# Attention probabilities made once in float32 and multiplied with float32 values, in a hybrid attention, long-convolution and expert layer

## The chip, the cores and the metric

The kernel runs on one core of a Trainium2 chip. The metric is the device time of one execution in microseconds (us), taken as the median of several runs of the same program. Each core has a matrix engine (TensorE, PE in the profile, with its weight loads shown apart as PEld), a vector engine (VectorE, DVE), an activation engine (ScalarE, ACT), a general engine (GpSimd, POOL) and a queue that issues transfers (SyncE, SP). Each engine takes its instructions in the order in which the program has them.

## The reference: what is computed

One layer over 1024 latent tokens of width 1024 with 256 context tokens. Tokens are normalised and modulated, projected to queries (8 heads of 64), keys and values (2 shared heads), three streams of a long convolution and two gates. Windowed attention and a two-step long convolution run side by side, their outputs are merged by the gates and projected, and a 32-expert layer (4 experts for each token) follows. The part that the change touches is the windowed attention of one block of 128 queries:

```python
s_loc = jnp.einsum('bqhgd,bshd->bhgqs', q_blk, k_blk).astype(jnp.float32) * scale
s_loc = jnp.where(valid, s_loc, -jnp.inf)
s_c = jnp.einsum('bqhgd,bchd->bhgqc', q_blk, k_ctx).astype(jnp.float32) * scale
p = jax.nn.softmax(jnp.concatenate([s_loc, s_c, s_sink], axis=-1), axis=-1).astype(v.dtype)
o = (jnp.einsum('bhgqs,bshd->bqhgd', p[..., :span], v_blk)
     + jnp.einsum('bhgqc,bchd->bqhgd', p[..., span:span + n_ctx], v_ctx))
```

Everything is float32. A query block looks at three key blocks of 128 around it (two at the ends) and at two blocks of context, and each head has a sink, a logit without a value.

## The kernel before

The program is written as generators that are advanced in turn, and a scheduler with its own model of durations then sets the order of each engine's instructions. Most products are float32 in effect: each operand is split into a float16 part and a float16 remainder, and three float16 matmuls (high by high, high by low, low by high) are summed in PSUM.

**Where the time goes, in order.** Up to about 300 us filters, layer norms and the convolution's input projections; from 300 to 664 us the long convolution (`hyena`, mostly on DVE) mixed with the value projection (`vproj`), the query and key projections (`qk`) and the gates (`gate`, line 821 by way of `proj`); from 664 to 884 us the attention, 4 query blocks alone and 4 mixed with the first half of the merge (`merge`, line 1102); from 884 to 928 us the second half of the merge; then the output projection (line 1143), the routing, and from about 1050 us the experts to the end.

**`vproj`** projects 10 tiles of 128 tokens (8 latent, 2 context). Line 890 (ACT) writes the high part of the values to `V`, line 891 (DVE) the remainder, both out of the same PSUM tile, of which there are three (`mm`). For each tile and shared head `V` holds 64 remainders, 64 high parts and a column of ones (129 float16 columns).

**`attn(g, i)`** treats the four heads of one shared head `g` for query block `i`; there are 16 such units, two for each block. Lines 997 and 998 make the scores with queries as rows, for the maximum alone (lines 999 to 1003, DVE); line 1007 (DVE) spreads the maxima to `Dm`. Then for each key block (4 or 5 of them, 76 in all units) lines 1013 to 1016 make the scores again, keys as rows and the four heads side by side (512 columns), less the maximum, in a PSUM tile `st` (`ff`, three of them). Line 1018 (ACT) takes the exponential to float16 (`ph`), line 1019 (ACT) the same exponential to float32 (`pe`), line 1020 (DVE) the difference to float16 (`pl`). Lines 1026 to 1028 multiply with the values, with the probabilities as weights (128 keys by 128 queries, loaded anew for each matmul) and the values as the moving operand (65 or 64 columns), into `O` (`tp`): three matmuls for each head and key block. The column of ones gives the denominators, which lines 1030 to 1032 (DVE) apply. After both units of a block four transposes (line 1041) bring the result to `aT`.

Two other float32 products on TensorE are of use below. Line 573 has a weight of 2 columns and 128 moving columns, and line 1061 has a weight of 128 columns and 1 moving column. Line 902 and line 1041 are float32 transposes.

Of the kernel before, what the change touches and what calls it, by code (L numbers as in the profile page):

```python
# [13 lines left out]
F32 = mybir.dt.float32  # L14
F16 = mybir.dt.float16
# [3 lines left out]
AF = mybir.ActivationFunctionType  # L19
ALU = mybir.AluOpType  # L20
# [494 lines left out]
class PhaseA:  # L515
# [364 lines left out]
    def vproj(s):  # L880
        nc=s.nc
        w=s.wsplit(640)
        nc.gpsimd.memset(s.V[:,:,:,128:129],1.0)
        for t in range(10):
            p=s.pmm()[:,:128]; i=0
            for k in range(8):
                for a,b in ((0,0),(0,1),(1,0)):
                    nc.tensor.matmul(p,s.hx[a][:,k,t*128:(t+1)*128],w[b][:,k,:],start=i==0,stop=i==23); i+=1
            pv=p.rearrange("p (g d) -> p g d",g=2)
            nc.scalar.activation(s.V[:,t,:,64:128],pv,AF.Copy,scale=2.**-6)  # L890
            nc.vector.scalar_tensor_tensor(s.V[:,t,:,0:64],pv,2.**-6,s.V[:,t,:,64:128],op0=ALU.mult,op1=ALU.subtract)
            if t%2==1: yield

    def hyena(s,hf,o,z):
# [65 lines left out]
class PhaseA2(PhaseA):  # L960
# [21 lines left out]
    def attn(s,wk,g,i,att):  # L982

        nc=s.nc
        qs=slice(i%2*128,i%2*128+128); hs=slice(4*g,4*g+4)
        loc=[j for j in (i-1,i,i+1) if 0<=j<8]
        keys=[(j*128,j) for j in loc]+[(1024,8),(1152,9)]
        mx=wk.tile([128,2,4],F32,name="mx",bufs=2)
        p2=s.pmm().rearrange("p (h k) -> p h k",h=4)
        nl=len(loc)+1  # L990
        for h in range(4):
            p=s.pmm()
            qh=s.Q2[i//2][0][0:64,4*g+h,qs]
            for n,(o,j) in enumerate(keys):
                dst=p[:,n*128:(n+1)*128] if n<nl else p2[:,h,:]
                msk=s.mlt if j==i-1 else s.mgt if (j==i+1 and j<8) else None
                nc.tensor.matmul(dst,qh,s.K2[0:64,g,o:o+128],start=True,stop=msk is None)  # L997
                if msk is not None: nc.tensor.matmul(dst,s.idb,msk,start=False,stop=True)
            nc.vector.tensor_reduce(out=mx[:,0,h:h+1],in_=p[:,:nl*128],axis=AX.X,op=ALU.max)
        nc.vector.tensor_reduce(out=mx[:,1,:],in_=p2,axis=AX.X,op=ALU.max)  # L1000
        m=wk.tile([128,4],F32,name="m4",bufs=2); mb=wk.tile([128,4],BF,name="mb",bufs=2)
        nc.vector.tensor_tensor(m,mx[:,0],mx[:,1],op=ALU.max)
        nc.vector.tensor_tensor(mb,m,s.sink[:,hs],op=ALU.max)
        nc.vector.tensor_tensor(m,s.sink[:,hs],mb,op=ALU.subtract)
        es=wk.tile([128,4],F32,name="es",bufs=2); nc.scalar.activation(es,m,AF.Exp)
        Dm=wk.tile([128,4,128],BF,name="Dm",bufs=2)
        nc.vector.tensor_tensor(Dm,s.nidb[:,None,:].to_broadcast([128,4,128]),mb[:,:,None].to_broadcast([128,4,128]),op=ALU.mult)
        O=s.ptp()[:,:4*65].rearrange("p (h c) -> p h c",h=4)
        P=[]
        for n,(o,j) in enumerate(keys):  # L1010
            st=s.pff().rearrange("p a b -> p (a b)").rearrange("p (h q) -> p h q",h=4)
            msk=s.mgt if j==i-1 else s.mlt if (j==i+1 and j<8) else None
            nc.tensor.matmul(st,s.K2[:,g,o:o+128],s.Q2[i//2][0][:,hs,qs],start=True,stop=False)
            nc.tensor.matmul(st,s.K2[:,g,o:o+128],s.Q2[i//2][1][:,hs,qs],start=False,stop=False)
            if msk is not None: nc.tensor.matmul(st,s.idb,msk[:,None,:].to_broadcast([128,4,128]),start=False,stop=False)
            nc.tensor.matmul(st,s.onb,Dm,start=False,stop=True)
            pe=wk.tile([128,4,128],F32,name="pe",bufs=2); ph=wk.tile([128,4,128],F16,name="ph",bufs=6); pl=wk.tile([128,4,128],F16,name="pl",bufs=6)
            nc.scalar.activation(ph,st,AF.Exp)
            nc.scalar.activation(pe,st,AF.Exp)
            (nc.gpsimd if n in s.plp else nc.vector).tensor_tensor(pl,pe,ph,op=ALU.subtract)  # L1020
            P.append((j,ph,pl))
        L=len(P)-1
        for h in range(4):
            d=O[:,h]
            for n,(j,ph,pl) in enumerate(P):
                nc.tensor.matmul(d,ph[:,h,:],s.V[:,j,g,64:129],start=n==0,stop=False)
                nc.tensor.matmul(d[:,0:64],ph[:,h,:],s.V[:,j,g,0:64],start=False,stop=False)
                nc.tensor.matmul(d,pl[:,h,:],s.V[:,j,g,64:129],start=False,stop=n==L)
        den=wk.tile([128,4],F32,name="den",bufs=2)
        nc.vector.tensor_tensor(den,O[:,:,64],es,op=ALU.add)  # L1030
        nc.vector.reciprocal(den,den)
        nc.vector.tensor_tensor(att[:,4*g:4*g+4,:],O[:,:,0:64],den[:,:,None].to_broadcast([128,4,64]),op=ALU.mult)
# [208 lines left out]
def build(nc,tc,A,out,dbg=None,nexp=32):  # L1241
    with ExitStack() as es:
# [3 lines left out]
        with ExitStack() as ea:  # L1246
            ec=ExitStack(); a=PhaseA2(nc,tc,A,ea,ec,dp); a.accD=accD; a.out=out; a.idb_,a.mcp=m.idf,m.cp
            a.HTd=dp.tile([2,128,4,1024],F16,name="HTd"); a.rowD=dp.tile([3,1024],F32,name="rowD")
            a.usepool,a.poolw=False,False
            a.V=a.cp.tile([128,10,2,129],F16,name="V")  # L1250
            E=lambda name,side="left": tc.tile_pool(name=name,bufs=1,side=side)
            eF,eK,eL,eP,eZ,eS,eQ,eA,eT=[ExitStack() for _ in range(9)]
            dq=lambda n:A[n].rearrange("h b a c k -> b h (a c k)").rearrange("b h (a c k) -> b h a c k",a=8,c=2)
# [139 lines left out]
```

## Time and profile before

| | us |
|---|---|
| three runs | 2492.09, 2493.93, 2496.49 (median 2493.93) |
| profiled execution | 2488.39, span 2486.6 |
| PE busy | 2196.3 (88%) |
| DVE busy | 2139.5 (86%) |
| ACT busy | 1466.0 (59%) |
| the three value matmuls, 304 each, lines 1026 to 1028, in 664 to 884 us | 36.3, 36.2 and 35.2 busy |
| the two exponentials, 76 each, in 664 to 884 us | 45.4 and 45.2 busy |
| the difference `pl`, 76, in 664 to 884 us | 51.3 busy |

Busy time of an engine is the union of its instructions' records. A matmul's record runs from its start to its result, so matmuls that follow each other closely overlap: what one of them occupies is read from the distance of the starts, not from its duration.

### The profile page before, as it was taken

The page shows a single profiled execution, that of the slowest core. Times are in us where ns is not written, and L with a number is a line of the kernel's source. Part 1 is how long each engine was busy: PE and PEld are TensorE (multiplying, and loading weights), DVE is VectorE, ACT ScalarE, POOL GpSimd, SP SyncE. Part 2 cuts the span into 40 slices and gives each one's busy share as a digit, 9 for nine tenths or more (in the row PEclk, how much of TensorE's full clock was granted, in tenths as well). Part 3 has the DMA queues.
Part 4 walks back from the last instruction along what each step waited for, and adds up shares of the span by engine and source line. Part 5 has one row for each costly group of instructions (what it writes and reads, how often), then busy time and mean ns, then how long its engine had stood idle before and what let it go on. Part 6 is the DMA issues. An engine that isn't in the chain of part 4 may idle for free.

```text
span 2486.6 us, 60718 instructions
## 1 busy us (share of the span) xinstructions
PE 2196.3 (88%) x25072; PEld 1650.7 (66%) x25073; DVE 2139.5 (86%) x4004; ACT 1466.0 (59%) x2185; POOL 347.6 (14%) x224
## 2 busy tenths in 40 slices
PE   7888999997498999569899989998989999999991
PEld 4555465444254544345666768898989999999991
DVE  6878897987978846869889988999999999999984
ACT  3543344223246413356867758697877878788882
POOL 0000001000000005201021021322041111221114
PEclk9899999999599999779898989998999999999995
DMA  8425546543314233288999989999999999999984
GB/s 288 136 85 171 194 139 180 168 163 114 87 18 136 81 119 129 90 280 280 306 293 310 313 286 332 330 331 329 340 327 349 337 343 336 353 349 358 349 273 154
DMA packets 520402, 594.25 MB, mean 239 GB/s; under 512 B 16708, under 2 KB 472332, under 8 KB 520118
## 3 DMA queue, kind: packets, MB, share of 16 engines
q1 hardware_dynamic: 493432, 508.27, 61.0%
q0 software_dynamic: 13152, 43.69, 6.9%
q10 hardware_dynamic: 13534, 38.35, 4.5%
q8 instruction: 198, 3.24, 0.5%
q14 instruction: 86, 0.70, 0.1%
HBM read 532.95 MB, written 57.29 MB: 237 GB/s over the span
## 4 chain that ended last, share of the span: by engine, by line
PE 45%; DVE 25%; DMA 8%; issue 7%; ACT 4%; POOL 3%; SPq 0%; DVEq 0%; POOLq 0%; ACTq 0%
PE acc L347 26%; DVE wl L317 8%; PE mm L1102 4%; PE mm L821 3%; DVE bf L731 3%; DMA g<-rows,gi 2%; PE acc L344 2%; DMA raw<-in_exp_w 2%; ACT wh L315 2%; DMA bf<-Hd 1%; DMA accD<-yr,si 1%; PE mm L997 1%; DVE sl L394 1%; PE yt L434 1%; DVE sg L393 1%
## 5 line engine op out<-in xcount | busy, mean ns | idle before, releaser
L317 DVE SCALAR_TENSOR_TENSOR wl<-raw,wh 128x1024 f16<-128x1024 f32 x768 | 910.0, 1216 | 56.4 <-ACT wh L315 53.5
L315 ACT ACTIVATE wh<-raw 128x1024 f16<-128x1024 f32 x768 | 768.2, 1049 | 183.1 <-PE acc L347 73.4
L347 PEld LDWEIGHTS <-wh 128*128 128x128 f16 x9984 | 785.6, 99 | 93.2 <-issue 17.4
L347 PE MATMUL acc<-xT,wh 128*128 128x80 f16 (+18 forms) x6656 | 718.7, 236 | 4.1 <-DVE yT L421 2.2
L347 PE MATMUL acc<-xT,wl 128*128 128x112 f16 (+19 forms) x3328 | 638.7, 235 | 0.4 <-issue 0.4
L347 PEld LDWEIGHTS <-wl 128*128 128x128 f16 x4992 | 493.0, 99 | 46.8 <-issue 10.7
L347 PE MATMUL acc<-ah,wh 128*128 128x112 f16 (+19 forms) x1664 | 329.8, 239 | 12.4 <-ACT ah L403 5.6
L347 PE MATMUL acc<-al,wh 128*128 128x112 f16 (+19 forms) x1664 | 330.6, 239 | 6.6 <-DVE al L404 6.5
L347 PE MATMUL acc<-ah,wl 128*128 128x112 f16 (+19 forms) x1664 | 330.4, 240 | 0.0
L821 PE MATMUL mm<-hx,wh 128*128 128x512 f16 (+1 forms) x1072 | 325.6, 382 | 4.6 <-DVE hx L636 4.0
L437 POOL DMA_INDIRECT accD<-yr,si x49 | 127.5, 2602 | 667.6 <-ACT yr L436 416.7
L821 PE MATMUL mm<-hx,wl 128*128 128x512 f16 x536 | 205.2, 383 | 2.7 <-DVE wl L808 2.7
L821 PEld LDWEIGHTS <-wh 128*128 128x128 f16 x1072 | 105.9, 99 | 118.6 <-issue 7.5
L277 POOL DMA_INDIRECT g<-rows,gi x44 | 119.4, 2714 | 462.2 <-DVE tf L266 418.5
L731 DVE TENSOR_TENSOR bf<-bf 128x256 f32<-128x256 f32 (+1 forms) x272 | 131.5, 541 | 0.3
L422 ACT ACTIVATE yT<-acc,bc,g2s 128x112 f32<-128x112 f32 (+19 forms) x208 | 97.7, 482 | 27.3 <-PE acc L347 27.2
L821 PEld LDWEIGHTS <-wl 128*128 128x128 f16 x536 | 53.0, 99 | 70.3 <-issue 10.2
L403 ACT ACTIVATE ah<-sl 128x64 f16<-128x64 f32 (+18 forms) x140 | 56.7, 409 | 52.8 <-DVE sl L399 52.5
L344 PEld LDWEIGHTS <-wl 128*128 128x128 f16 x1152 | 79.6, 99 | 12.0 <-issue 10.5
L344 PEld LDWEIGHTS <-wh 128*128 128x128 f16 x1152 | 81.4, 104 | 6.8 <-DVE yT L421 4.7
L393 DVE TENSOR_SCALAR sg<-acc,bc 128x112 f32<-128x112 f32 (+19 forms) x208 | 75.4, 378 | 11.4 <-PE acc L347 11.4
L394 DVE TENSOR_SCALAR sl<-acc,bc 128x112 f32<-128x112 f32 (+19 forms) x208 | 75.3, 377 | 10.9 <-PE acc L347 10.5
(399 smaller groups left out, 3574.6 us busy)
## 6 DMA issues: line engine op xcount, KB each, us to landing
raw<-in_exp_w SPq DMA_DIRECT2D x384, 1024.0 KB
wr<-in_w_in SPq DMA_DIRECT2D x34, 512.0 KB
t<-in_w_mod ACTq DMA_DIRECT2D x32, 512.0 KB
bf<-in_dec SPq DMA_DIRECT2D x32, 256.0 KB
Hd<-bf ACTq DMA_DIRECT2D x32, 256.0 KB
bf<-Hd SPq DMA_DIRECT2D x32, 256.0 KB
Gd<-t ACTq DMA_DIRECT2D x16, 512.0 KB
gt<-Gd SPq DMA_DIRECT2D x32, 256.0 KB
```

Source lines behind the costliest of these rows:

```text
L277: nc.gpsimd.indirect_dma_start(out=g[:cs].rearrange("p a d -> p (a d)"),out_offset=None,in_=s.rows,in_offset=bass.IndirectOffsetOnAxis(ap= ...
L315: else: nc.scalar.activation(wh[:,o],raw[:,o],AF.Copy,scale=sc)
L317: else: nc.vector.scalar_tensor_tensor(wl[:,o],raw[:,o],64.0,wh[:,o],op0=ALU.mult,op1=ALU.subtract)
L344: nc.tensor.matmul(ps_,wh,x[k],start=k==0,stop=False); nc.tensor.matmul(ps_[:,0],wl,x[k][:,0],start=False,stop=k==7)
L347: nc.tensor.matmul(ps_,a,b,start=n==0,stop=n==23); n+=1
L393: nc.vector.tensor_scalar(g[:,j],pg[:,j],bc[:,f:f+1],448.0,op0=ALU.add,op1=ALU.min)
L394: nc.vector.tensor_scalar(l[:,j],pl[:,j],bc[:,8+f:9+f],512.0,op0=ALU.add,op1=ALU.min)
L422: nc.scalar.activation(y,py,AF.Identity,bias=bc[:,16+m:17+m],scale=s.g2s[:,m:m+1])
L437: st=nc.gpsimd.indirect_dma_start(out=s.accD,out_offset=bass.IndirectOffsetOnAxis(ap=si[:cs,:1],axis=0),in_=yr[:cs],in_offset=None,compute ...
L731: (nc.gpsimd if pool and s.usepool else nc.vector).tensor_tensor(o,a,b,op=op)
L821: nc.tensor.matmul(p,w[a][:,k,:],s.hx[b][:,k,o],start=i==0,stop=i==23); i+=1
L1102: nc.tensor.matmul(p,w[a_][:,k,m*128:(m+1)*128],X[x][:,k,o] if b==0 else X[x][:,k,:],start=n==0,stop=n==11); n+=1
```

## The change

`V` becomes float32 with 65 columns (64 values and the ones): line 890 writes the float32 values and line 891 is gone. In `attn` lines 1018 and 1020 are gone: the exponential is taken once, to float32, in six buffers in place of two. The three float16 matmuls of a head and a key block become one matmul with a float32 weight (128 by 128) and 65 float32 moving columns.

```diff
--- before.py
+++ after.py
@@ -880,15 +880,14 @@
     def vproj(s):
         nc=s.nc
         w=s.wsplit(640)
-        nc.gpsimd.memset(s.V[:,:,:,128:129],1.0)
+        nc.gpsimd.memset(s.V[:,:,:,64:65],1.0)
         for t in range(10):
             p=s.pmm()[:,:128]; i=0
             for k in range(8):
                 for a,b in ((0,0),(0,1),(1,0)):
                     nc.tensor.matmul(p,s.hx[a][:,k,t*128:(t+1)*128],w[b][:,k,:],start=i==0,stop=i==23); i+=1
             pv=p.rearrange("p (g d) -> p g d",g=2)
-            nc.scalar.activation(s.V[:,t,:,64:128],pv,AF.Copy,scale=2.**-6)
-            nc.vector.scalar_tensor_tensor(s.V[:,t,:,0:64],pv,2.**-6,s.V[:,t,:,64:128],op0=ALU.mult,op1=ALU.subtract)
+            nc.scalar.activation(s.V[:,t,:,0:64],pv,AF.Copy,scale=2.**-6)
             if t%2==1: yield
 
     def hyena(s,hf,o,z):
@@ -1014,18 +1013,12 @@
             nc.tensor.matmul(st,s.K2[:,g,o:o+128],s.Q2[i//2][1][:,hs,qs],start=False,stop=False)
             if msk is not None: nc.tensor.matmul(st,s.idb,msk[:,None,:].to_broadcast([128,4,128]),start=False,stop=False)
             nc.tensor.matmul(st,s.onb,Dm,start=False,stop=True)
-            pe=wk.tile([128,4,128],F32,name="pe",bufs=2); ph=wk.tile([128,4,128],F16,name="ph",bufs=6); pl=wk.tile([128,4,128],F16,name="pl",bufs=6)
-            nc.scalar.activation(ph,st,AF.Exp)
+            pe=wk.tile([128,4,128],F32,name="pe",bufs=6)
             nc.scalar.activation(pe,st,AF.Exp)
-            (nc.gpsimd if n in s.plp else nc.vector).tensor_tensor(pl,pe,ph,op=ALU.subtract)
-            P.append((j,ph,pl))
+            P.append((j,pe))
         L=len(P)-1
         for h in range(4):
-            d=O[:,h]
-            for n,(j,ph,pl) in enumerate(P):
-                nc.tensor.matmul(d,ph[:,h,:],s.V[:,j,g,64:129],start=n==0,stop=False)
-                nc.tensor.matmul(d[:,0:64],ph[:,h,:],s.V[:,j,g,0:64],start=False,stop=False)
-                nc.tensor.matmul(d,pl[:,h,:],s.V[:,j,g,64:129],start=False,stop=n==L)
+            for n,(j,pe) in enumerate(P): nc.tensor.matmul(O[:,h],pe[:,h,:],s.V[:,j,g,:],start=n==0,stop=n==L)
         den=wk.tile([128,4],F32,name="den",bufs=2)
         nc.vector.tensor_tensor(den,O[:,:,64],es,op=ALU.add)
         nc.vector.reciprocal(den,den)
@@ -1247,7 +1240,7 @@
             ec=ExitStack(); a=PhaseA2(nc,tc,A,ea,ec,dp); a.accD=accD; a.out=out; a.idb_,a.mcp=m.idf,m.cp
             a.HTd=dp.tile([2,128,4,1024],F16,name="HTd"); a.rowD=dp.tile([3,1024],F32,name="rowD")
             a.usepool,a.poolw=False,False
-            a.V=a.cp.tile([128,10,2,129],F16,name="V")
+            a.V=a.cp.tile([128,10,2,65],F32,name="V")
             E=lambda name,side="left": tc.tile_pool(name=name,bufs=1,side=side)
             eF,eK,eL,eP,eZ,eS,eQ,eA,eT=[ExitStack() for _ in range(9)]
             dq=lambda n:A[n].rearrange("h b a c k -> b h (a c k)").rearrange("b h (a c k) -> b h a c k",a=8,c=2)
```

Lines behind 890 move up by one, and behind the exponential by seven, so that line 1026 of before is line 1021 of after. The scheduler also moves other instructions between 300 and 930 us; on PE the last 32,625 instructions, with the whole expert part among them, stand in the same order in both.

On PE, at the end of a unit's value product, before: `ph` and `pl` are the probabilities, `att` the finished block, `K` and `Q` the next scores.

```order
L1026 LDWEIGHTS ph
L1026 MATMUL tp<-V,ph 128x65
L1027 LDWEIGHTS ph
L1027 MATMUL tp<-V,ph 128x64
L1028 LDWEIGHTS pl
L1028 MATMUL tp<-V,pl 128x65
L1041 MATMUL tp<-idf,att 128x128 x2
L1013 LDWEIGHTS K_4555
L1013 MATMUL ff<-Q_4558,K_4555 128x512
L1014 LDWEIGHTS K_4555
```

After, at the like place (`pe` is the probabilities; a float32 matmul loads its own weight and stands as one row):

```order
L996 LDWEIGHTS Q_6818
L996 MATMUL mm<-K_4545,Q_6818 128x128
L1021 MATMUL tp<-V,pe 128x65 x16
L1012 LDWEIGHTS K_4545
L1012 MATMUL ff<-Q_6818,K_4545 128x512
L1013 LDWEIGHTS K_4545
L1013 MATMUL ff<-Q_6819,K_4545 128x512
```

Of three rows of load and matmul for each head and key block one is left, 16 of them in a row here, between the maxima's scores and the next block's scores.

On ACT, about the third unit, before (`es` is the sink's exponential):

```order
L1005 ACTIVATE es<-m_6746 128x4
L1018 ACTIVATE ph<-ff 128x512 x2
L1019 ACTIVATE pe<-ff 128x512 x2
L1018 ACTIVATE ph<-ff 128x512
L1019 ACTIVATE pe<-ff 128x512
L1018 ACTIVATE ph<-ff 128x512
L1019 ACTIVATE pe<-ff 128x512
```

After:

```order
L1004 ACTIVATE es<-m_6538 128x4
L1017 ACTIVATE pe<-ff 128x512 x3
L1004 ACTIVATE es<-m_6640 128x4
L1017 ACTIVATE pe<-ff 128x512 x7
L1036 ACTIVATE aT_6415<-tp 128x4x128
L1004 ACTIVATE es<-m_6745 128x4
L1017 ACTIVATE pe<-ff 128x512 x5
```

Each key block has one exponential where it had two, and `aT`, the output of a finished query block, comes earlier in the row.

## Rows read from the trace of the kernel before

**Rows 1.** The page: span, engines, PE's busy tenths in 40 slices.

```profile
span 2486.6 us, 60718 instructions
...
PE 2196.3 (88%) x25072; PEld 1650.7 (66%) x25073; DVE 2139.5 (86%) x4004; ACT 1466.0 (59%) x2185; POOL 347.6 (14%) x224
...
PE   7888999997498999569899989998989999999991
```

**Rows 2.** Windows: stretch, length, busy of each engine (count), PE clock, DMA.

```profile
884.00:928.00 44.00, 44.00 (x191) 19.30 (x191) 19.42 (x29) 4.42 (x7) 0.00 (x0) 0.93 0.34 121
664.00:884.00 220.00, 200.95 (x1793) 107.97 (x1793) 175.24 (x337) 108.30 (x203) 0.00 (x0) 0.92 0.32 91
```

**Rows 3.** The chain that ended last, 664 to 884 us, shares by line.

```profile
by line: PE mm L1102 20.3%; PE mm L997 14.4%; PE ff L1013 8.2%; PE mm L998 7.5%; PE ff L1016 6.9%; PE ff L1014 6.7%; PE tp L1028 4.6%; PE tp L1026 4.0%; PE tp L1027 3.7%; DMA big<-in_w_branch_attn 3.4%; DMA hT<-HTd 2.9%; PE ff L1015 2.6%; A
```

**Rows 4.** Waits, 664 to 884 us: who for whom, us, times, longest.

```profile
PE ff L1013 <- ACT pe L1019: 6.0, 6, 2.0
...
PE mm L1102 <- DMA hT<-HTd: 2.9, 1, 2.9
...
PE mm L997 <- DMA Q<-QD: 2.2, 1, 2.2
...
PE tp L1026 <- ACT ph L1018: 2.0, 1, 2.0
...
PE tp L1028 <- DVE pl L1020: 0.8, 2, 0.6
```

**Rows 5.** Timeline of PE, 693.2 to 694.3 us: start, us, instruction.

```profile
693.23 0.20 PE L1026 MATMUL tp<-V,ph 128*128 128x65 f16 x1
...
694.25 0.19 PE L1026 MATMUL tp<-V,ph 128*128 128x65 f16 x1
```

**Rows 6.** Instructions by line, 664 to 884 us: busy, mean ns, idle before.

```profile
L1020 DVE TENSOR_TENSOR pl<-pe,ph 128x512 f16<-128x512 f32 x76 | 51.3, 682 | 4.3 <-ACT pe L1019 4.0
...
L1018 ACT ACTIVATE ph<-ff 128x512 f16<-128x512 f32 x76 | 45.4, 606 | 41.7 <-PE ff L1016 21.9 <-PE tp L1027 19.5
L1019 ACT ACTIVATE pe<-ff 128x512 f32<-128x512 f32 x76 | 45.2, 607 | 6.8 <-DVE pl L1020 6.6
```

**Rows 7.** Line 573, its matmuls; then a run of them in the PE timeline.

```profile
L573 PE MATMUL mm<-hx,S x160: 272/273/421, 21.9 to 46.1; 128*2 128x128 f32 x160
```

```profile
40.24 1.91 PE L573 MATMUL mm<-hx,S 128*2 128x128 f32 x16
```

**Rows 8.** Line 1061, its instructions (ns: least, median, most); then its loads, PEld timeline.

```profile
L1061 PEld LDWEIGHTS tp<-ones,t x16: 190/192/192, 368.0 to 369.9; 128*128 128x128 f32 x16
L1061 PE MATMUL tp<-ones,t x16: 169/250/250, 368.0 to 369.9; 128*128 128x1 f32 x16
```

```profile
368.40 1.64 PEld L1061 LDWEIGHTS tp<-ones,t 128*128 128x128 f32 x14
```

**Rows 9.** Line 902, its instructions; then a pair of its matmuls in the PE timeline.

```profile
L902 PEld LDWEIGHTS tp<-idf,z x64: 186/188/254, 205.2 to 590.8; 128*128 128x128 f32 x64
L902 PE MATMUL tp<-idf,z x64: 272/273/378, 205.5 to 590.9; 128*128 128x128 f32 x64
```

```profile
205.45 0.38 PE L902 MATMUL tp<-idf,z 128*128 128x128 f32 x2
```

**Rows 10.** Line 888's idle time before it; the chain by line, 300 to 340 us.

```profile
  DVE V L891: 5.4, 4
```

```profile
by line: DVE t L1057 19.4%; DVE bf L731 14.0%; DVE bf L922 11.0%; issue 10.7%; DVE bf L920 10.3%; DVE t L842 6.2%; DVE t L841 6.0%; DVE wl L806 5.9%; DVE bf L919 5.0%; DVE V L891 4.7%; ACT t L839 3.6%; DVE wl L808 2.8%; ACT u L838 1.7%; DVE
```

**Rows 11.** Windows: two of the attention, then those of rows 8 and 5.

```profile
668.00:685.00 17.00, 15.67 (x75) 6.57 (x74) 12.66 (x29) 6.95 (x15) 0.00 (x0) 0.50 0.74 151
720.00:752.00 32.00, 31.19 (x284) 17.06 (x284) 26.30 (x59) 15.74 (x33) 0.00 (x0) 1.00 0.00 1
...
367.90:370.20 2.30, 2.30 (x25) 2.19 (x23) 2.30 (x3) 1.62 (x3) 0.09 (x1) 1.00 0.12 36
693.20:694.30 1.10, 1.10 (x38) 1.10 (x37) 0.98 (x4) 1.05 (x4) 0.00 (x0) 1.00 0.00 0
```

## The prediction

> **What bounds the kernel now.** The page comes first: PE is busy in 88% of the span and DVE in 86%, and PE's slices read 8 or 9 nearly everywhere [rows 1]. Such averages don't say which engine ends a stage, so I go to the stage that the change rewrites, 664 to 884 us. In the windows PE is busy for 200.95 of its 220 us, DVE for 175.24 and ACT for 108.30 [rows 2]. The chain by line decides between them: of its first twelve shares ten are lines of TensorE (20.3, 14.4, 8.2, 7.5, 6.9, 6.7, 4.6, 4.0, 3.7 and 2.6, together 78.9%), two are transfers with 6.3%, and no line of DVE or ACT is among them [rows 3]. So the stage runs at the pace of PE's own row of instructions. The waits view says what is left: PE's largest idle pieces are 6.0 us for `pe` (an exponential that has to free a PSUM tile), 2.0 us for `ph`, 0.8 us for `pl`, and two transfers with 2.9 and 2.2 us [rows 4]. Behind the stage comes the second half of the merge, in which PE is busy for all 44.00 of 44 us [rows 2]; it needs the last query blocks, and from there on PE's row is the same in both kernels. So a shift at 884 us should reach the end whole.
>
> The change is therefore priced on PE first. What it takes from DVE and ACT counts only as far as PE was waiting for them.
>
> **What it removes.** *On PE* 912 float16 matmuls, three for each of 304 pairs of head and key block. In the timeline line 1026 starts at 693.23 and, eleven periods later, at 694.25 [rows 5]: 1.02 us / 11 = 93 ns for three loads and three matmuls. 304 x 93 ns = **28.3 us** of PE. (The records of 190 to 200 ns each overlap; their busy time, 36 us for a line, is no price.) *On ACT* one exponential of 606 ns for each of 76 key blocks, 76 x 0.606 = 46.1 us (busy 45.4). *On DVE* 76 differences of 682 ns, 51.8 us (busy 51.3) [rows 6]. The chain does not pass through either, so of these 98 us I count only the PE waits named above, 6.0 + 2.0 + 0.8 = **8.8 us**: with one exponential for each tile in place of two, the tile is free after half the time. That is the most that these rows give. Bounds are nothing, since the wait for `pe` can also come from ACT standing at a weight that hasn't landed (3.4% of the chain, 7.5 us, is a transfer for line 1085 [rows 3]), and some 9 us more, since waits shorter than the tail of a matmul's record don't show as idle.
>
> *In `vproj`* line 891 goes, ten operations that shared their PSUM tile with PE. PE stood 5.4 us for it, while the chain of 300 to 340 us lay on DVE, with line 891 at 4.7% of 40 us, 1.9 us [rows 10]. I take half of the 5.4, **2.7 us**; the bounds are nothing (the convolution on DVE ends the stage anyway) and 5.4.
>
> **What it adds.** 304 float32 matmuls with a weight of 128 columns and 65 moving columns. No such pair stands in the trace, but both of its sides do.
>
> *How many passes.* Line 1061 has 8 float32 matmuls in the program and 16 records of load and matmul in the trace [rows 8]: each is run in two passes, each with a load of its own. So 608 passes.
>
> *The moving side.* Line 573 moves 128 float32 columns over a weight of 2: 16 matmuls in 1.91 us, the last of 0.272, so (1.91 - 0.27) / 15 = 109 ns a pass [rows 7], and 65 columns need 65/128 of it, 55 ns. A matmul would be 111 ns, 304 of them 33.7 us: only 5.4 us more than before.
>
> *The weight side.* Line 1061 moves one column, so its period is the load: 14 loads in 1.64 us, the last of 0.192, (1.64 - 0.19) / 13 = 111 ns for 128 float32 columns [rows 8]. By contrast a float16 load, a matmul and all fit in 93 / 3 = 31 ns [rows 5]. The granted clock is 1.00, the upper level of 2.4 GHz, in both places [rows 11].
>
> *Together.* Line 902 shows a load and a matmul at once: loads recorded with 188 ns (line 1061: 192) between matmuls that follow at 0.38 - 0.27 = 0.11 us, which is what their 128 moving columns need alone [rows 9, 7]. The load lies beside the matmul before it, and a pass costs the longer of the two sides. Here that is the load: 111 ns, not 55. A matmul costs 222 ns, 304 of them **67.5 us**. Bounds: 33.7 us if the load were hidden wholly, and 608 x (111 + 55) = 100.9 us if the two stood one behind the other. I take the value between, since line 1061 has the very weight in question.
>
> The Trainium skill, FP8 and Floating Point Precision, section TensorE Precision Notes, prices true float32 otherwise: four passes through the array. An estimate by that page alone would set four against three and give 304 x 93 x 4/3 = 37.7 us, 9.4 more than before, near my lower bound. The trace agrees with it on the moving side alone: two passes at twice the time for a column. The loads of rows 8 speak against it as a price here.
>
> A new wait: the value matmuls now depend on the one exponential, which is ready 606 ns after the scores where `pl` took 606 + 607 + 682 ns, so nothing is late for that. Six buffers of `pe` stand where six of `ph` and `pl` stood. Behind the longer value runs (3.6 us for 16 matmuls, where 48 float16 ones took 1.5) the next scores stand in PE's row, and with them the maxima on DVE and the exponentials on ACT; both have more room than before (175 - 52 and 108 - 46 us of work in a longer stage).
>
> **The sum.** PE: 67.5 - 28.3 = +39.2 us. Waits: -8.8. `vproj`: -2.7. Together **+28 us**. Against the profiled execution of 2488.4 us that is 2516; this execution lies 5.5 us below the median of the three runs, 2493.9, and beside that median the forecast is **2522 us**. The bounds of the small terms add or take some 12 us. Upwards there is also the clock: the stage's granted clock is 0.92 of full, and 17 us of it lay at the lower level (0.50 [rows 11]), where a pass costs twice as much; value matmuls that fall there add up to 5 us.
>
> **The rivals.**
>
> *Not slower: the load hides.* If the load of the next weight runs ahead over several matmuls, or is cheaper in this mix, a pass costs its moving side, 55 ns: +5.4 - 8.8 - 2.7 = -6 us, 2488. It decides below (28.3 + 8.8 + 2.7) us / 608 = 65 ns a pass. For it: the float16 loads here do hide, and DVE and ACT lose 98 us of work. Against it: line 1061's loads had nothing to wait for and still came every 111 ns.
>
> *Much slower: load and matmul in turn.* A pass of 166 ns gives 100.9 - 28.3 - 11.5 = +61, 2555. For it: in a run where loads are the longer side no row shows a wide matmul beside them. Against it: rows 9.
>
> *The clock falls.* In the value runs the array is fed for 55 ns of 111. If the clock were granted at the lower level for half of these 67.5 us, that half would take twice as long, +34 on top, 2556. For it: the level of 0.50 in 668 to 685 us, though PE counts as busy for 15.67 of 17 us there. Against it: 1.00 throughout 720 to 752 us, with much the same mixture [rows 11].
>
> *The change does less than it says*, if a float32 matmul were run as one pass: then 304 x 111 = 33.7 us, the first rival's price by another way; rows 8 speak against it.
>
> **How the numbers follow.** The forecast has 0.72, its own range 2510 to 2539 by the small terms and the value matmuls at the lower level; the load that hides, by either way, 0.11; load and matmul in turn 0.08; the falling clock 0.09. The range goes from 2504, where a pass hides a tenth of its load as well (100 ns for 111, 6.7 us), to 2550, which takes in a clock that falls for two fifths of the value runs (+27); it leaves out the first rival and the ends of the other two. What a measurement can tell from no change is about 0.2%, 5 us: the first rival lies at its edge, with 0.07 beyond and 0.04 within. Faster 0.07, same 0.04, slower 0.89.
>
> **What would show it.** Line 1021 of the new kernel should have 608 records of load and of matmul, a run of 16 matmuls (32 passes) should last some 3.6 us, and the passes should start 111 ns apart: 55 would be the first rival, 166 the second, 222 the clock. PE's share in 664 to 884 us and what follows should rise, ACT's and DVE's work there should fall by 46 and 52 us, and the waits for `pe` should shrink. The merge's second half should start some 28 us later, at about 912 us, with the expert part behind it as long as before. It would be wrong if the stage's chain turned out to lie on something other than PE, or if the new order of the scheduler moved a transfer (the queries, the branch weights) onto it.

## The result, and the profile after

| | before | after |
|---|---|---|
| median of four runs on one chip, us | 2495.21 (2492.09 to 2497.68) | 2536.07 (2534.64 to 2540.13) |
| profiled execution, us | 2488.39 | 2540.13 |
| convolution ends (last start of its last DVE line), us | 663.1 | 674.2 |
| output projection starts on PE, us | 928.1 | 976.1 |

The change makes the kernel slower: 1.0167 times the time before, interval 1.0149 to 1.0185. Run again beside e5, e6 and e7 below, the same kernel had 2535.21 us, 1.0171 (1.0133 to 1.0208). The rise of the medians is 41 to 46 us, where the prediction had 28; 2536 us lies inside its range of 2504 to 2550. The two profiled executions, one of each kernel, lie 52 us apart. Of these 11 are there when the convolution ends (2 of them already at 300 us, where the rows of PE, DVE and ACT still have the same order in both), 37 more when the output projection starts, and 4 come in the experts.

The page of after, to be read beside [rows 1]: span, and busy time, share and instructions of each engine.

```profile
span 2538.4 us, 60025 instructions
...
PE 2235.1 (88%) x24768; PEld 1693.5 (67%) x24769; DVE 2096.9 (83%) x3918; ACT 1432.0 (56%) x2109; POOL 347.5 (14%) x224
```

PE is busy for 38.8 us more with 304 matmul records less; DVE and ACT are relieved of 42.6 and 34.0 us, and that buys little (e6 below).

The new matmul, line 1021 (least, median and most ns; first and last start), then one run of 26 passes in the timelines of PE and of its loads (start us, us, instruction):

```profile
L1021 PEld LDWEIGHTS tp<-V,pe x608: 186/192/337, 690.2 to 918.0; 128*128 128x128 f32 x152
L1021 PE MATMUL tp<-V,pe x608: 220/275/474, 690.6 to 918.1; 128*128 128x65 f32 x152
```

```profile
704.93 3.01 PE L1021 MATMUL tp<-V,pe 128*128 128x65 f32 x26
```

```profile
704.72 3.09 PEld L1021 LDWEIGHTS tp<-V,pe 128*128 128x128 f32 x26
```

608 records stand for 304 matmuls in the program. The run lasts 3.01 us; less the last record of 0.275 that is 2.74 / 25 = 110 ns from start to start, and the median distance over all of after's runs at the full clock is 112 ns. That is the load of [rows 8], 111 ns.

Two stretches of after in the windows view (length, busy of PE, PEld, DVE, ACT, POOL with counts, clock, DMA): attention and merge, to be held against [rows 2], and a piece of it:

```profile
672.00:976.00 304.00, 286.80 (x1690) 171.43 (x1688) 157.21 (x293) 78.89 (x134) 0.00 (x0) 0.90 0.28 85
...
734.50:762.00 27.50, 27.50 (x113) 16.14 (x112) 9.59 (x24) 5.07 (x11) 0.00 (x0) 0.50 0.00 1
```

PE is still the engine that sets the pace (286.80 of 304), by a wider margin than before. The second row is new: 27.5 us on end at the lower level of the clock, behind six microseconds, 728.6 to 734.5, in which PE ran little but scores for the maxima and their masks in turn. The longest such piece before was 17 us [rows 11]. Between the convolution's end and the output projection the clock stood at 0.50 for 41 us before and for 61 us after.

**Where the time of that stretch went.** To charge each matmul of PE with what it holds up, I took from the trace the distance from its start to the next matmul's start, so that a wait is charged to the matmul ahead of it. The sums from the convolution's end to the output projection, in us (the last two columns are for experiments below, e7 on after, e9 on before, both with one edit; in e9 21 of the 251 transposed scores stand ahead of the convolution's end and are not in its sum):

| | before | after | e7_full_rows | e9_before_full |
|---|---|---|---|---|
| value matmuls (1026 to 1028; 1021) | 43.4 | 72.5 | 72.3 | 47.4 |
| scores for the maxima and their masks (997, 998) | 58.9 | 61.6 | 39.3 | 41.1 |
| transposed scores (1013 to 1016) | 64.5 | 66.2 | 57.9 | 62.5 |
| merge, transposes and the rest | 97.2 | 100.6 | 89.9 | 94.1 |
| sum | 264.0 | 300.9 | 259.4 | 245.1 |

The value matmuls rose by 29.1. The other rows rose by 7.8, though their instructions are the same in number: 3.9 of it is the wait for one transfer, `hT`, which grew from the 2.9 us of [rows 4] to 6.8, and the longer stay at the lower clock comes beside it. Waits of PE in after, 672 to 976 us (us, times, longest):

```profile
PE mm L1095 <- DMA hT<-HTd: 6.8, 1, 6.8
...
PE mm L996 <- DVE mx L998: 2.2, 2, 1.9
```

The 6.0 us that PE waited for `pe` are gone from this view.

### The profile page after: what moved, and what is told of

It reads as the page before. It is cut to its first block, busy times and chain, and to the rows that moved or that the text cites. A ratio compares the mean times of both kernels' runs of the same rounds, so it can differ in the third digit from the quotient of the medians.

```text
span 2538.4 us, 60025 instructions
## 1 busy us (share of the span) xinstructions
PE 2235.1 (88%) x24768; PEld 1693.5 (67%) x24769; DVE 2096.9 (83%) x3918; ACT 1432.0 (56%) x2109; POOL 347.5 (14%) x224
## 4 chain that ended last, share of the span: by engine, by line
PE 48%; DVE 26%; DMA 7%; issue 5%; ACT 3%; POOL 2%; SPq 0%; DVEq 0%; ACTq 0%; POOLq 0%
PE acc L347 30%; DVE wl L317 8%; PE mm L821 3%; DVE bf L731 3%; PE mm L1095 3%; PE tp L1021 2%; DMA g<-rows,gi 2%; DMA t<-in_w_mod 1%; PE acc L344 1%; DMA accD<-yr,si 1%; PE yt L434 1%; DMA bf<-Hd 1%; PE mm L996 1%; DVE sl L394 1%; ACT wh L315 1%
## 5 line engine op out<-in xcount | busy, mean ns | idle before, releaser
L422 ACT ACTIVATE yT<-acc,bc,g2s 128x112 f32<-128x112 f32 (+19 forms) x208 | 97.9, 482 | 27.8 <-PE acc L347 27.5
L1017 ACT ACTIVATE pe<-ff 128x512 f32<-128x512 f32 x76 | 43.3, 595 | 89.5 <-PE ff L1015 65.6
L1021 PEld LDWEIGHTS tp<-V,pe 128*128 128x128 f32 x608 | 80.2, 202 | 7.7 <-issue 1.5
```

The lines of the kernel that those rows point to most:

```text
L422: nc.scalar.activation(y,py,AF.Identity,bias=bc[:,16+m:17+m],scale=s.g2s[:,m:m+1])
L1021: for n,(j,pe) in enumerate(P): nc.tensor.matmul(O[:,h],pe[:,h,:],s.V[:,j,g,:],start=n==0,stop=n==L)
```

## The experiments

They were run in three groups, each on one chip together with the kernel before: e1 to e4; after once more with e5, e6 and e7; e8, e9 and e10. Times are medians, with the ratio to the group's own before and its interval; kernels of different groups are best compared by their ratios. After is the base unless the text says before. Each edit can also change the order that the scheduler makes. The diffs are cut (`...`) to what matters.

**Does the load set the price of a pass, or load and matmul in turn?** e3 widens the moving side alone, from 65 to 128 columns (63 columns of the other shared head move as well and are not read), and the load stays.

```diff
...
-nc.tensor.matmul(O[:,h],pe[:,h,:],s.V[:,j,g,:],start=n==0,stop=n==L)
+nc.tensor.matmul(O[:,h],pe[:,h,:],Vw[:,j,:],start=n==0,stop=n==L)
...
```

> The changed kernel with 128 moving columns in each value matmul in place of 65 (63 columns of the other shared head are multiplied as well and not read). Theory A (the longer of the two sides): the moving side is 109 ns, the load 111, so nothing changes: 2536 us, from 2532 to 2542, passes 111 ns apart. The rival of the prediction (load and moving side one behind the other): 608 x 54 ns = 33 us more, 2569.

Measured: 2541.65 us, 1.0213 (1.0182 to 1.0244). Line 1021 and a run of the same 26 passes in PE's timeline:

```profile
L1021 PE MATMUL tp<-V,pe x608: 272/275/580, 691.0 to 919.5; 128*128 128x128 f32 x152
```

```profile
705.35 3.06 PE L1021 MATMUL tp<-V,pe 128*128 128x128 f32 x26
```

3.06 us where 65 columns took 3.01, and 112 ns as the median distance in both. With twice the columns at next to no price in a pass, the moving side lies beside the load: the rival of load and matmul in turn, which asked for 33 us more, is out. The whole time is some 6 us above both medians of after, at the upper end of what was expected, with intervals that overlap; the value matmuls hold 2 us of it (74.7 by the measure of the table above, for 72.5).

e2 halves the weight instead: 64 of a block's 128 queries are loaded, 65 columns move.

```diff
...
-nc.tensor.matmul(O[:,h],pe[:,h,:],s.V[:,j,g,:],start=n==0,stop=n==L)
+nc.tensor.matmul(O[0:64,h],pe[:,h,0:64],s.V[:,j,g,:],start=n==0,stop=n==L)
...
```

> The changed kernel with only 64 of the 128 queries as the weight of the value matmuls; the other half of each query block's output is left out (zeros). Theory A (a pass costs the longer of its load and its moving side): the load falls to 56 ns, about the 55 ns of the moving side, so 608 passes lose 55 ns each, 33 us: 2503 us, passes about 57 ns apart. Theory C (the loss of the change comes from the other row of instructions and a lower clock, not from the loads): within 8 us of the changed kernel, 2528 to 2536.

The other queries' results are zeros here, which sends tokens to other experts, so the whole time (3638.1 us, with an expert part of 2691) says nothing; it is read up to the output projection. From the convolution's end to there it took 273.6 us, against 301.9 and 302.4 in two traces of after: 28 us less, where 33 were expected. Line 1021's loads, and a run of 26 passes on PE with the matmul ahead of it:

```profile
L1021 PEld LDWEIGHTS tp<-V,pe x608: 132/138/232, 687.4 to 899.3; 128*64 128x64 f32 x152
```

```profile
700.46 0.38 PE L1013 MATMUL ff<-Q,K 128*128 128x512 f16 x1
700.77 1.73 PE L1021 MATMUL tp<-V,pe 128*64 128x65 f32 x26
```

(1.73 - 0.22) / 25 = 60 ns a pass. Half the load brings it to about the 55 ns that [rows 7] give for 65 moving columns. With e3 this settles it: a pass costs the longer of its sides, and in after that is the load. The 28 us are not the passes alone. By the measure of the table the value matmuls fell by 23.5 us (49.0 for 72.5) and not by 33. They now use 64 columns of the array, and each of 96 changes between them and matmuls over the whole array takes nearly 0.1 us more: above it is 0.31 us from a transposed score to the first pass, where after has 0.22. Against that the wait for `hT` was 0.8 us for 6.8.

**What was the relief of ACT and DVE worth?** e4 takes it without the float32 matmul: before, with one exponential, `ph` used in all three matmuls. e6 undoes it in after: the second exponential and the difference are made again and not read.

```diff
+ph=wk.tile([128,4,128],F16,name="ph",bufs=2); pl=wk.tile([128,4,128],F16,name="pl",bufs=2)
+nc.scalar.activation(ph,st,AF.Exp)
 nc.scalar.activation(pe,st,AF.Exp)
+nc.vector.tensor_tensor(pl,pe,ph,op=ALU.subtract)
```

> The kernel before without the second exponential and without the difference pl; the third float16 matmul takes the high part again, so the low part of the probabilities is left out. PE has the same 912 matmuls, ACT loses 46 us and DVE 52. Theory A (PE's row bounds the attention, and of this work only the waits of PE count, 8.8 us): 2486 us, from 2480 to 2492 beside 2495 of before. Rival (ACT and DVE are worth more than the chain shows): 2475 or less. Rival (the scheduler's new row, with 56 of the maxima's scores in one piece, loses at the clock what the waits give): 2493 to 2500.

> The changed kernel with the second exponential (ph) and the difference (pl) made as before and not read: the price on PE alone. Theory A (the removed work was worth 8.8 us of waits at most, and with the longer rows of weight loads PE covers most of it): 0 to 9 us above the changed kernel. Rival (the removed work is on the chain): 20 us or more above it.

e4: 2484.06 us, 0.9977 (0.9962 to 0.9993), 5 us less than before; attention and merge 258.5 us for 265.0. The waits went as the prediction had them: of the 8.8 us of PE for `pe`, `ph` and `pl` 0.5 are left. But the wait for `hT` grew from 2.9 to 7.3 us and the time at the lower clock from 41 to 55, which took part of it back. e6: 2538.03 us, 1.0184 (1.0145 to 1.0222), 2.8 us over the after that ran beside it, with intervals that overlap. So the prediction's 8.8 us were right as waits and brought some 5 net with float16 value matmuls. With the float32 ones, whose stage is longer, ACT and DVE have time for most of the extra work (4.3 us of waits for `pe` come back): the rival's 20 us are out, while anything from nothing to some 10 us would fit these runs.

**What did `vproj` do?** e1 puts a DVE operation back where line 891 stood; its result goes to a scratch tile that nothing reads.

```diff
 nc.scalar.activation(s.V[:,t,:,0:64],pv,AF.Copy,scale=2.**-6)
+nc.vector.scalar_tensor_tensor(s.vd,pv,2.**-6,s.V[:,t,:,0:64],op0=ALU.mult,op1=ALU.subtract)
...
```

> The changed kernel with line 891's operation put back in the value projection, its result written to a scratch tile and not read, so that up to the attention the engines' rows stand as in the kernel before, and in the attention nearly as in the changed one. Theory A (the longer rows of weight loads cost about 30 us in the attention, and the scheduler's other row of instructions in the convolution about 7 more, as the end of the convolution went from 663 to 674 us, with 3 to 4 us of that there already at 300 us): 2529 us, 7 less than the changed kernel. Theory B (those 7 us are the scatter of single executions, and the operation in vproj is worth the 2.7 us that the prediction gave): 2536 to 2539, and the convolution ends at about 674 us again.

2531.29 us, 1.0171 (1.0145 to 1.0197). The convolution's last line on DVE (16 operations; first and last start) in before, after and e1:

```profile
L946 DVE SCALAR_TENSOR_TENSOR z<-z,skip,ff x16: 1135/1148/1178, 367.7 to 663.1; 128x512 f32<-128x512 f32 x16
```

```profile
L945 DVE SCALAR_TENSOR_TENSOR z<-z,skip,ff x16: 1130/1144/1178, 371.4 to 674.2; 128x512 f32<-128x512 f32 x16
```

```profile
L946 DVE SCALAR_TENSOR_TENSOR z<-z,skip,ff x16: 1124/1139/1175, 359.0 to 659.3; 128x512 f32<-128x512 f32 x16
```

Ten operations less on DVE, and the convolution, which lies on DVE, ends 11 us later. In all seven traces with the operation in place (before, e1, e4, e5, e8, e9, e10) it ends between 659 and 665 us, in all six without it (two of after, e2, e3, e6, e7) between 670 and 676. Part of that is scatter: up to 300 us PE, DVE and ACT have the same order in all thirteen, and yet the matmul that starts at 299.9 us in before starts between 296.0 and 301.7 in the others. Counted from that matmul the convolution ends after 363 to 366 us with the operation and after 372 to 376 without it, so the operation is worth some 10 us there. Without it the scheduler sets another order between 300 and 670 us, in which DVE stands idle more: 56 to 59 us, counted in the same way, for 45 to 48. (e1's order is not that of before either, PE's rows part at about 330 us; it is the operation that both have in common.) DVE's waits for the transfers out of `Hd` (between 380 and 662 us; us, times, longest), in before, after and e1:

```profile
DVE bf L919 <- DMA bf<-Hd: 13.3, 4, 6.8
```

```profile
DVE bf L918 <- DMA bf<-Hd: 19.9, 6, 7.2
```

```profile
DVE bf L919 <- DMA bf<-Hd: 8.9, 3, 5.4
```

Between before and after that is 6.6 us (all of DVE's idle time there is 45, 53 and 41 us); which step of the new order makes these transfers late was not tried. Of the 15 us by which e1's trace is ahead of after's there, 5 stand at 300 us already, with the same order in both. Whether the other 10 reach the end these runs don't show: e1's attention and merge take 305.3 us, 65 of them at the lower clock, its experts 1563.7 where after has 1562.3 and 1558.8, its median is 4 to 5 us below the two of after, and its ratio to before is the same, 1.0171 beside 1.0167 and 1.0171. After was run once more for this. Expected were 51 us above before and 8 to 10 above e1 if the order reaches the end, or 41 to 43 above before if all of it is scatter; the 46 us measured lie between. In e10 below the same edit does reach the end.

**The scores for the maxima.** The table above shows a cost that the prediction never looked at. These scores are contracted over 64 rows of the array, and many of them stand next to a mask over 128. PE's timeline in after:

```profile
730.77 0.23 PE L997 MATMUL mm<-mlt,idb 128*128 128x128 bf16 x1
730.93 0.28 PE L996 MATMUL mm<-K,Q 64*128 64x128 f16 x2
731.14 0.23 PE L997 MATMUL mm<-mgt,idb 128*128 128x128 bf16 x1
731.31 0.51 PE L996 MATMUL mm<-K,Q 64*128 64x128 f16 x6
731.74 0.23 PE L997 MATMUL mm<-mlt,idb 128*128 128x128 bf16 x1
```

A mask to the next score 162 ns, a score to the next 66, a score to a mask 149 (medians over the stage, at the upper clock). e7 contracts the scores over all 128 rows, which hold the queries twice and the keys' remainders beside their high parts; it adds a small term to the maximum, whose choice cancels in the softmax.

```diff
-qh=s.Q2[i//2][0][0:64,4*g+h,qs]
+qh=s.Q2[i//2][0][:,4*g+h,qs]
-nc.tensor.matmul(dst,qh,s.K2[0:64,g,o:o+128],start=True,stop=msk is None)
+nc.tensor.matmul(dst,qh,s.K2[:,g,o:o+128],start=True,stop=msk is None)
```

> The changed kernel, with the maxima's scores (lines 995 to 997) contracted over all 128 rows (the low half of the keys is added) in place of 64. The changed kernel's granted clock is 0.50 from 734.5 to 762 us, behind a run of 56 such scores in a row. Theory D (that run, with half the array's rows, is what brings the clock down there, and the time at the lower clock costs some 10 us): the clock stays at 1.00 behind the run, and the time is 6 to 12 us under the changed kernel. Rival (the rows don't matter, the run's many small matmuls do): the clock falls as before and the time is the same within 3 us.

2496.52 us, 1.0019 (0.9998 to 1.0040): 39 us below the after that ran beside it (2535.21), and level with before. I had expected 6 to 12. The timeline:

```profile
720.11 0.22 PE L997 MATMUL mm<-mlt,idb 128*128 128x128 bf16 x1
720.16 0.27 PE L996 MATMUL mm<-K,Q 128*128 128x128 f16 x2
720.27 0.22 PE L997 MATMUL mm<-mgt,idb 128*128 128x128 bf16 x1
720.33 0.28 PE L996 MATMUL mm<-K,Q 128*128 128x128 f16 x2
720.44 0.22 PE L997 MATMUL mm<-mlt,idb 128*128 128x128 bf16 x1
```

From mask to mask, with two scores between, it is 0.16 to 0.17 us where after has 0.37: among scores and masks each matmul now follows the one before at 56 ns (median). And the clock, attention and merge of e7:

```profile
669.00:932.00 263.00, 243.67 (x1695) 163.47 (x1692) 154.92 (x293) 79.16 (x134) 0.00 (x0) 0.97 0.34 98
```

0.97 for 0.90; the lower level holds for 17 us in place of 61. In the table the scores and masks fall by 22.3 us, the other rows by 19.2. Of these 6.8 are the wait for `hT`, which e7 does not have; the rest comes by the clock and by transposed scores that stand next to scores. Whether the clock rose because of the full rows or because PE had less of such waiting between matmuls, and why `hT` is no longer waited for, these runs don't tell.

e9 makes the same edit in before, e10 adds e1's edit to e7.

> The kernel before with the maxima's scores contracted over all 128 rows, and nothing else. In e7 the start of a score behind a mask came 56 ns after the mask's in place of 162, that of a mask behind a score 56 in place of 149, and the time at the lower clock between convolution and output projection fell from 61 to 17 us. Theory D (both belong to the 64-row matmuls, whatever follows): some 220 such changes of rows at about 100 ns are 22 us, and 41 us at the lower clock fall to under 20, another 5 to 12 us: 2455 to 2463 us beside 2489 of before. Rival (e7 gains only in the changed kernel, where long rows of loads follow): 2480 or more.

> e7 with line 891's operation put back in the value projection as in e1: upstream rows as before. Theory A (the other row of the convolution costs some 10 us at the convolution's end, of which e1 kept 4): the convolution ends at 659 to 665 us in place of 671.5, and the time is 4 to 10 us under e7's 2496.5. Rival (upstream is scatter): same as e7 within 3 us.

e9: 2469.70 us, 0.9917 (0.9891 to 0.9944), the fastest kernel of the study that leaves nothing out. It is 22 us below the before that ran beside it (2492.13), where some 26 to 34 below 2489 were expected. Its attention and merge, and two of PE's waits in it:

```profile
659.00:907.00 248.00, 213.68 (x1971) 124.71 (x1990) 195.60 (x369) 113.04 (x210) 0.00 (x0) 0.94 0.36 104
```

```profile
PE ff L1013 <- ACT pe L1019: 8.1, 13, 2.4
PE tp L1028 <- DVE pl L1020: 5.4, 8, 1.2
```

PE is idle for 34 of 248 us, where e7 leaves it 19 of 263: with cheap value matmuls and cheap scores PE waits more for DVE (195.60 us busy) and ACT. e10: 2485.09 us, 0.9980 (0.9964 to 0.9996); its convolution ends at 662.1 us, and it lies 11 us below e7 by the medians, 10 by the ratios, so here `vproj`'s order reaches the end whole. With line 891's operation and the full rows in both, what is left of the change costs 2485.09 - 2469.70 = 15.4 us.

**A cheaper way to one exponential?** e5 is before with one float16 exponential and two float16 matmuls for each head and key block; the probabilities' remainder is dropped. e8 is e5 with full rows.

```diff
...
 nc.tensor.matmul(d,ph[:,h,:],s.V[:,j,g,64:129],start=n==0,stop=False)
-nc.tensor.matmul(d[:,0:64],ph[:,h,:],s.V[:,j,g,0:64],start=False,stop=False)
-nc.tensor.matmul(d,pl[:,h,:],s.V[:,j,g,64:129],start=False,stop=n==L)
+nc.tensor.matmul(d[:,0:64],ph[:,h,:],s.V[:,j,g,0:64],start=False,stop=n==L)
```

> The kernel before with one exponential, to float16, and two matmuls for each head and key block (ones and high values, low values): the low part of the probabilities is left out. PE loses 304 float16 matmuls of 31 ns, 9.4 us, ACT 46 and DVE 52 us. Theory A: e4's gain of 5 to 7 us and 9.4 more, 14 to 16 us under before. Rival (the scheduler's new row loses it at the clock): not more than e4, 5 us under before.

> e5 (one exponential to float16, two value matmuls, the low part of the probabilities left out) with the maxima's scores over all 128 rows. If the two gains add, e9's and e5's 8 us: about 2447 us, from 2440 to 2458. If PE is no longer what ends the attention, e9's time, 2455 to 2463.

e5: 2481.53 us, 0.9956 (0.9937 to 0.9975), 8 to 11 us below before, where 14 to 16 were expected. e8: 2448.78, 0.9832 (0.9808 to 0.9855), as expected, and 21 us below e9. A third of the value matmuls is 304 x 31 ns = 9.4 us of that. The rest fits the relief of ACT and DVE: PE's waits for `pe`, `ph` and `pl`, 13.7 us in e9, are 0.6 in e8, against a wait of 6.3 us for `hT` that e9 does not have. No run takes the two apart; e4 with full rows was not run.

## Why the prediction was right, and where it was not

- **The sign and the mechanism were right**, and 2536 us lies in the range, 14 above the forecast. The stage runs at PE's pace, one pass costs the float32 load, and there are two passes to a matmul: 608 records, 110 to 112 ns apart, as the prediction's 111. Both rivals on the price are out: the load that hides by the 112 ns themselves, load and matmul in turn by e3.
- **The value matmuls and their waits together** were put at 39.2 - 8.8 = +30.4 us and measured +29.1, as charged in the table. That it agrees so closely is partly luck, for both ends are higher than put. After has 72.5 for 67.5: 608 x 112 ns is 68 us, and 40 passes at the lower clock, 213 ns apart, add 4, as the text allowed ("up to 5 us"). Before has 43.4 for 28.3 + 8.8 = 37.1: beside its waits for `pe` (5 us), `ph` and `pl`, which are gone in after, its row holds one of 2.4 us for the queries' transfer and more.
- **`vproj` had the wrong sign.** The term was -2.7 us, with bounds of nothing and 5.4, and the step that failed is that the loss of line 891 could at worst change nothing, since "the convolution on DVE ends the stage anyway". It does, but in the order that the scheduler makes without line 891 it ends 9 to 12 us later, counted from 300 us. The prediction named a moved transfer as what would make it wrong, yet gave it no price in the sum. At the convolution's end this is 12 to 15 us against the sum, of the 13 to 18 by which it fell short. How much of it lasts to the end is open in after itself (e1); between e7 and e10 all of it does.
- **The clock was priced on the wrong instructions.** Only value matmuls at the lower level were counted, and only 17 us at that level, where the 0.92 of [rows 2] over 220 us makes some 35 (0.08 x 220 / 0.50). The level of 0.50 lasted 61 us for 41. It doubles what a matmul over 128 rows takes (427 ns for 216, 213 for 112), while scores and masks take a quarter to two thirds more (82 for 66, 222 for 162, 243 for 149). The table's other rows hold +7.8 us, of which 3.9 is the wait for `hT`; the value matmuls' own share is the 4 us above. The rival that the clock falls in the value runs did not come about: none of the four pieces at the lower level in after begins behind such a run, and the longest begins among the scores.
- **What it foretold of the stage**: the output projection behind the merge starts 48 us later in these two traces (976.1 for 928.1), where 28 were foretold; the experts took 1562.3 and 1558.8 us for 1558.5. ACT fell by 34.0 us and not 46: exponentials that follow each other start 478 ns apart, not their recorded 606, and 76 x 478 ns is 36 us. DVE fell by 42.6, with line 891 gone as well, where 52 were foretold: the instruction behind a difference starts 602 ns after it, not the recorded 682. The text had warned of such overlap for PE's records and then summed those of ACT and DVE.

## What to carry to other kernels

Price a matmul by the longer of its load and its moving side, each read from a run in which the other is short; few moving columns over a full float32 weight pay for the load alone, and in a stage that runs at TensorE's pace work taken from other engines is no exchange for it. Measure what a removed instruction does to the order, not only its own time: here ten cheap operations less on DVE made a stage end some 10 us later. And before replacing the arithmetic of a stage, charge every matmul in it with the distance to the next: the largest saving here stood in a line that the change did not touch.

## What was not expected of the hardware

A matmul over 64 rows next to one over 128 rows costs about 93 to 106 ns more than two over 128: 149 and 162 ns from start to start for 56, and 312 for 216 from a transposed score of 512 columns to a score. Between two scores of 64 rows it is 66 ns, so most of it is the change of height and not the height. e2 shows the like for columns: its value matmuls use 64 columns of the array, and from a transposed score to such a pass it is 309 ns for 216, from such a pass to a transposed score 154 for 112 (medians, e2 and after). And the granted clock went with the rows: in the changed kernel 61 us at the lower level became 17, in the kernel before 41 became 27.
